# The low part of split weights, made by a negation on ScalarE and an accumulating transfer instead of subtractions

## The chip, the cores and the metric

The kernel runs on one core of a Trainium2 chip. The metric is the device time of one execution in microseconds. The engines are named as the profile names them: PE (TensorE, with PEld for its weight loads), DVE (VectorE), ACT (ScalarE), POOL (GpSimd) and SP (SyncE, which here only issues transfers).

## What is computed

The reference is one inference step of a two-layer hybrid backbone over 128 context tokens and 512 latent tokens, 640 in all, with D = 1024 and a feed-forward width of 2816. Every layer runs four token mixers on the same normalised input, merges them through gates, projects, and runs a SwiGLU feed-forward:

```python
h = _rmsnorm(x, lp['norm1_g']) * (1.0 + sc1) + sh1
(aq, ak, av, az, aa, ab, ..., mg) = jnp.split(h @ lp['w_in'], offs, axis=-1)
...                                      # four mixers: DeltaNet, differential attention, HGRN2, neighbourhood attention
proj = jnp.einsum('btnw,nwd->btnd', branches, lp['w_branch'])
gates = jax.nn.sigmoid(mg.reshape(bsz, t, N_BRANCH, D_MODEL))
out = jnp.einsum('btnd,btnd->btd', gates, proj) @ lp['w_out']
x = x + g1 * out
h = _rmsnorm(x, lp['norm2_g']) * (1.0 + sc2) + sh2
x = x + g2 * (jax.nn.silu(h @ wg) * (h @ wu)) @ wd
```

All of it is in 32-bit floats. The change concerns the weights of these products: `w_in`, `w_branch`, `w_out`, `wg`, `wu` and `wd`.

## The kernel before

**Split products.** TensorE multiplies in a reduced format (F32R). So each operand is split in two, a high part (the value rounded to that format) and a low part (the value minus its high part), and a product is the sum of three matmuls: high by high, high by low of the activations, low of the weights by high. `unit` does that for one half of the tokens (320 columns) and up to 8 steps of 128 rows: 24 matmuls of 320 columns for one weight tile of 128x1024. `units` does both halves at once. Activations are kept split (`hh`, `hl`, `fa`, `mo`, `mgs`); weights are streamed.

**Weights.** `load_w` brings one weight tile: a transfer on SP's queue into `wraw` (2 buffers), the copy to the high part `whi` on ACT (3 buffers), and the low part `wlo` (3 buffers, `NLO`) as a subtraction. In the mixers (`self.weaving`) the last 416 of 1024 columns (`PC`) are subtracted on POOL and the first 608 on DVE; elsewhere DVE does all of it. `load_spare` does the same into other tiles for a few weights that have to be kept, and is not touched. The callers of `load_w` are `first` (three tiles of the opening), `a_small` (`in_wab`, 128 columns), `store_fm` and `store_tok` (the input projection, the latter with two tiles held at a time), `pregate` and `merge` (gates and branch projections), the loop over `in_wo` in `build` (the output projection, one tile for each half of the tokens), and `ffn` (`up`: gate and up tiles of 1024 columns; `down`: tiles of 512 columns, in one chunk 256).

**Order.** In the mixers TensorE's order is written out by a planner (`weave`), which puts steps of the mixers' chains between the matmuls of the projections; it is part of the program and is not changed at run time. The other engines' orders are made by a scheduler from priorities; what `load_w` issues has a high one (`WPRI`). Each engine and each issuing queue works strictly in its order. POOL's queue also carries transfers of the differential attention (`rr`, `rx`, `bqk`, `bqt`, `bKd`), SP's queue nearly all others.

**Stages.** For each layer: the mixers with the input projection, then the output projection, then the feed-forward, where `up` of one chunk of columns is followed by `down` of the chunk before it. The first layer begins with `first`; the modulation of the second layer is computed on DVE during the first layer's feed-forward.

Of the kernel before, what the change touches and what calls it, by code (L numbers as in the profile page):

```python
# [12 lines left out]
ALU = mybir.AluOpType  # L13
# [24 lines left out]
WPRI, WCUT = 550000, 1024  # L38
QB = 1
RE = 0  # L40
PC = 416
DPRI = 0
QM, QD = 1, 0
VC = 1
# [69 lines left out]
class Net:  # L114
# [58 lines left out]
    def weave(self, chains, fill, side):  # L173
# [25 lines left out]
        while chains or fill or side:  # L199
            first = None  # L200
            for group, margin in ((side, 0.0), (chains, SLACK), (fill, 0.0)):
                pick = None
                for c in group:
                    t = ready(c)
                    if t is not None:
                        if t + margin <= self.now:
                            pick = c
                            break
                        first = t + margin if first is None else min(first, t + margin)
                if pick is None:  # L210
                    continue
                if group is chains:
                    self.chain, self.rank = True, pick[2]
                    with self.tc.high_priority(offset=100000 * (8 - self.rank)):
                        step(pick, group)
                    self.chain = False
                else:

                    group.insert(0, group.pop(group.index(pick)))
                    step(pick, group)  # L220
                break
            else:
                assert first is not None, "chains wait for each other"
                self.now = first
# [50 lines left out]
            lo.append(l)  # L275
        return Halves(hi, 512), Halves(lo, 512)

    def load_w(self, src, n=1024, pc=0, raw=None):

        if raw is None:  # L280
            raw = self.wraw.tile([128, 1024], F32, tag="raw", name="wraw")
        with self.tc.high_priority(offset=DPRI):
            self.nc.sync.dma_start(raw[:, :n], src)
        hi = self.whl.tile([128, 1024], F32R, tag="hi", name="whi")
        lo = self.whl.tile([128, 1024], F32R, tag="lo", name="wlo", bufs=NLO)
        with self.tc.high_priority(offset=WPRI):
            m = n - (PC if self.weaving and n == 1024 else pc)
            self.a.copy(hi[:, :n], raw[:, :n])
            self.v.tensor_tensor(lo[:, :m], raw[:, :m], hi[:, :m].bitcast(F32), ALU.subtract)
            if m < n:  # L290
                self.g.tensor_tensor(lo[:, m:n], raw[:, m:n], hi[:, m:n].bitcast(F32), ALU.subtract)
        return hi, lo
# [223 lines left out]
    def first(self, xs, mod, ms_):  # L516
# [11 lines left out]
        wide, wa, shifts, ws = [], [], {}, []  # L528
# [31 lines left out]
                    v.tensor_tensor(accs[j], accs[j], sq, ALU.add)  # L560
        for m in ms_:
            raw = self.mo.tile([128, 2, T], F32, tag="mo", name="wa0").rearrange("p a b -> p (a b)") if len(ws) == 2 else None
            ws.append(self.load_w(self.I['win'][0, m], pc=512, raw=raw))
        w1 = []
        for n in range(8):
            w1.append(self.SA("wa2"))
# [81 lines left out]
        n = 0  # L648
# [1308 lines left out]
```

## Time and profile before

| | |
|---|---|
| Median of 3 runs | 3494.56 us (3494.28 to 3498.4) |
| The profiled execution | 3495.59 us, of which the span is 3493.6 us |
| Mean granted clock of TensorE | 0.984 of full speed |
| PE busy | 3368.8 us (96 %) |
| DVE busy | 2352.5 us (67 %) |
| ACT busy | 1422.4 us (41 %) |
| POOL busy | 544.5 us (16 %) |
| Transfers | 460.16 MB, mean 132 GB/s |

Busy time is the time in which an engine executes an instruction; issuing a transfer is not counted. The span runs from the first instruction to the last; the 2.0 us around it belong to the execution as a whole. The mixers of the first layer run to about 1210 us, its output projection from 1231 to 1288, its feed-forward to about 1770; the second layer's mixers end at about 2920 and its feed-forward at the end.

### The profile page before, as it was taken

The page shows a single profiled execution, that of the slowest core. Times are in us where ns is not written, and L with a number is a line of the kernel's source. Part 1 is how long each engine was busy: PE and PEld are TensorE (multiplying, and loading weights), DVE is VectorE, ACT ScalarE, POOL GpSimd, SP SyncE. Part 2 cuts the span into 40 slices and gives each one's busy share as a digit, 9 for nine tenths or more (in the row PEclk, how much of TensorE's full clock was granted, in tenths as well). Part 3 has the DMA queues.
Part 4 walks back from the last instruction along what each step waited for, and adds up shares of the span by engine and source line. Part 5 has one row for each costly group of instructions (what it writes and reads, how often), then busy time and mean ns, then how long its engine had stood idle before and what let it go on. Part 6 is the DMA issues. An engine that isn't in the chain of part 4 may idle for free. (4 is left out here: it accounts for less than half of the span.)

```text
span 3493.6 us, 63588 instructions
## 1 busy us (share of the span) xinstructions
PE 3368.8 (96%) x23932; PEld 3298.6 (94%) x23932; DVE 2352.5 (67%) x5497; ACT 1422.4 (41%) x3170; POOL 544.5 (16%) x592
## 2 busy tenths in 40 slices
PE   8999999989999999999999999999999999999998
PEld 5989999988999999999999899999999999999998
DVE  7689888865676478887456797777555646633435
ACT  5344444544543353222253455445544433522222
POOL 2221112422122100000002212124122121000000
PEclk9999999999999999999999999999999999999999
DMA  6444333855454254444244333348453235322222
GB/s 218 151 145 139 115 110 124 242 178 159 131 154 126 95 177 147 151 153 131 76 131 148 130 115 112 103 127 244 141 150 120 87 100 161 106 67 79 74 84 67
DMA packets 297931, 460.16 MB, mean 132 GB/s; under 512 B 48148, under 2 KB 193172, under 8 KB 297624
## 3 DMA queue, kind: packets, MB, share of 16 engines
q1 hardware_dynamic: 286296, 423.58, 39.3%
q0 software_dynamic: 11328, 32.52, 3.1%
q8 instruction: 189, 3.10, 0.4%
q14 instruction: 118, 0.97, 0.1%
HBM read 368.42 MB, written 87.56 MB: 131 GB/s over the span
## 5 line engine op out<-in xcount | busy, mean ns | idle before, releaser
L152 PE MATMUL pu<-hh,whi 128*128 128x320 f32 (+1 forms) x3760 | 1094.7, 319 | 18.1 <-ACT stg L107 14.9
L152 PE MATMUL pu<-hl,whi 128*128 128x320 f32 (+1 forms) x3760 | 1064.8, 311 | 2.2 <-DVE hl L107 2.2
L152 PE MATMUL pu<-hh,wlo 128*128 128x320 f32 (+1 forms) x3760 | 1065.2, 311 | 0.0
L107 ACT CAST whi<-wraw 128x1024 fp32r<-128x1024 f32 (+2 forms) x410 | 391.1, 954 | 898.0 <-PE pu L152 492.6
L152 PEld LDWEIGHTS pu<-hh,whi 128*128 128x128 f32 (+1 forms) x3760 | 683.9, 189 | 23.3 <-ACT stg L107 15.7
L152 PEld LDWEIGHTS pu<-hl,whi 128*128 128x128 f32 (+1 forms) x3760 | 684.3, 189 | 4.5 <-DVE hl L107 2.5
L152 PEld LDWEIGHTS pu<-hh,wlo 128*128 128x128 f32 (+1 forms) x3760 | 682.5, 188 | 1.7
L107 DVE TENSOR_TENSOR wlo<-wraw,whi 128x608 fp32r<-128x608 f32 (+3 forms) x410 | 389.7, 951 | 314.2 <-ACT whi L107 309.4
L107 POOL TENSOR_TENSOR wlo<-wraw,whi 128x416 fp32r<-128x416 f32 (+1 forms) x209 | 325.5, 1558 | 1761.1 <-ACT whi L107 1539.8
L152 PE MATMUL pu<-mo,whi 128*128 128x320 f32 x1024 | 236.5, 318 | 5.4 <-DVE mo L107 3.4
L152 PE MATMUL pu<-fa,whi 128*128 128x320 f32 x1152 | 215.6, 309 | 0.0
L107 DVE SCALAR_TENSOR_TENSOR x<-pu,gn,x 128x128 f32<-128x128 f32 (+1 forms) x336 | 133.8, 435 | 93.3 <-PE pu L152 92.4
L152 PE MATMUL ptk<-whi,hh 128*128 128x256 f32 x640 | 193.9, 303 | 0.0
L512 DVE CUSTOM_DVE_ANT_0 junk<-wa,cs,mod 128x256 bf16<-128x256 f32 (+1 forms) x288 | 172.7, 600 | 25.6 <-DMA wa<-in_wada 20.7
L152 PE MATMUL ptk<-wlo,hh 128*128 128x256 f32 x640 | 183.5, 287 | 3.2 <-DVE wlo L107 3.2
L152 PE MATMUL ptk<-whi,hl 128*128 128x256 f32 x640 | 183.4, 287 | 0.0
L152 PEld LDWEIGHTS pu<-mo,whi 128*128 128x128 f32 x1024 | 174.5, 193 | 7.6 <-DVE mo L107 4.9
L152 PEld LDWEIGHTS pu<-fa,whi 128*128 128x128 f32 x1152 | 180.8, 188 | 0.0
L152 PE MATMUL pu<-mo,wlo 128*128 128x320 f32 x512 | 160.7, 314 | 0.0
L152 PE MATMUL pu<-fa,wlo 128*128 128x320 f32 x576 | 131.1, 309 | 0.0
L152 PEld LDWEIGHTS ptk<-wlo,hh 128*128 128x128 f32 x640 | 125.2, 196 | 3.4 <-DVE wlo L107 3.4
L152 PEld LDWEIGHTS ptk<-whi,hh 128*128 128x128 f32 x640 | 125.5, 196 | 0.0
(422 smaller groups left out, 6092.1 us busy)
## 6 DMA issues: line engine op xcount, KB each, us to landing
wraw<-in_win SPq DMA_DIRECT2D x151, 512.0 KB, 3.9
wa<-in_wada SPq DMA_DIRECT2D x116, 256.0 KB, 3.0
wraw<-in_wg SPq DMA_DIRECT2D x44, 512.0 KB, 3.5
wraw<-in_wu SPq DMA_DIRECT2D x44, 512.0 KB, 3.7
wraw<-in_wd SPq DMA_DIRECT2D x80, 256.0 KB, 2.6
p<-stg SPq DMA_DIRECT2D x112, 160.0 KB, 2.9
wa<-in_wada SPq DMA_DIRECT2D x128, 128.0 KB, 2.5
wraw<-in_wtok SPq DMA_DIRECT2D x32, 512.0 KB, 3.8
```

The lines of the kernel that those rows point to most:

```text
L107: r = f(*args, **kw)
L152: r = self.nc.tensor.matmul(out, lhsT, rhs, start=start, stop=stop)
L512: self.nc.vector.tensor_tensor_reduce(junk, raw, cs[g], 0.5, o if k0 else self.bada[:, l, m:m + 1], ALU.mult, ALU.add, o)
```

## The change

`load_w` gets a second way, used by all callers but `first`. ACT writes the negated weights into the low tile, which rounds them to F32R, so the tile holds minus the high part. A transfer issued by POOL then reads the same weights from DRAM once more and adds them to the tile. ACT's copy to the high part stays. The constant `PC` is gone, since neither DVE nor POOL subtracts in this way.

```diff
-PC = 416
...
-    def load_w(self, src, n=1024, pc=0, raw=None):
+    def load_w(self, src, n=1024, pc=0, raw=None, add=True):
...
+        if add:
+            with self.tc.high_priority(offset=WPRI):
+                self.a.mul(lo[:, :n], raw[:, :n], -1.0)
+                self.nc.gpsimd.dma_start(lo[:, :n], src, accum_op=ALU.add)
+                self.a.copy(hi[:, :n], raw[:, :n])
+            return hi, lo
         with self.tc.high_priority(offset=WPRI):
-            m = n - (PC if self.weaving and n == 1024 else pc)
+            m = n - pc
...
-            ws.append(self.load_w(self.I['win'][0, m], pc=512, raw=raw))
+            ws.append(self.load_w(self.I['win'][0, m], pc=512, raw=raw, add=False))
```

408 tiles take the new way: 326 of 1024 columns, 64 of 512, 16 of 256 and 2 of 128, together 189.9 MB. TensorE's order is the same up to the first layer's output projection. ACT's order at the beginning of that projection, before (`mgh` are the last of the merged activations, `sq` the squares for the next norm, `wraw` here the tiles of `in_wo`):

```order
L107 CAST mgh_14778<-mrg_11837 128x320
L107 CAST whi_14860<-wraw_14858 128x1024
L107 CAST mgh_14779<-mrg_11837 128x320
L107 CAST whi_14895<-wraw_14893 128x1024
L107 ACTIVATE sq_15067<-x_14786 128x320
L107 CAST whi_14930<-wraw_14928 128x1024
L107 ACTIVATE sq_15069<-x_14821 128x320
```

ACT at the same place now:

```order
L106 CAST whi_14863<-wraw_14861 128x1024
L106 ACTIVATE wlo_14864<-wraw_14861 128x1024
L106 CAST mgh_14780<-mrg_11838 128x320
L106 CAST whi_14899<-wraw_14897 128x1024
L106 ACTIVATE wlo_14900<-wraw_14897 128x1024
L106 ACTIVATE sq_15076<-x_14787 128x320
L106 CAST whi_14935<-wraw_14933 128x1024
L106 ACTIVATE wlo_14936<-wraw_14933 128x1024
```

Each copy to a high part now has the negation of the same tile right behind it, and the work of the norm stands behind both. POOL's order in the first layer's mixers, where it issues the transfers of the differential attention, before:

```order
L163 DMA bqt_7740<-bqk0_102 64x4x128 x2
L163 DMA bKd_7737<-bqk0_102 128x512
L163 DMA bKd_7738<-bqk0_102 128x512
L107 MEMSET dpr_7760 128x256
L163 DMA rr_7518<-qk2_96 32x2x512 x2
L107 TENSOR_TENSOR wlo_8063<-wraw_8060,whi_8062 128x416
L107 TENSOR_TENSOR wlo_8186<-wraw_8183,whi_8185 128x416
L107 TENSOR_TENSOR wlo_8339<-wraw_8336,whi_8338 128x416
L163 DMA bqk2_104<-rr_7518 64x512 x4
L163 DMA rr_7536<-qk3_97 32x2x512 x3
```

POOL at the same place now:

```order
L162 DMA bqt_7741<-bqk0_102 64x4x128 x2
L162 DMA bKd_7738<-bqk0_102 128x512
L162 DMA bKd_7739<-bqk0_102 128x512
L106 MEMSET dpr_7761 128x256
L162 DMA rr_7519<-qk2_96 32x2x512
L288 DMA wlo_8064<-in_win 128x1024
L162 DMA rr_7519<-qk2_96 32x2x512 x2
L288 DMA wlo_8187<-in_win 128x1024
L288 DMA wlo_8340<-in_win 128x1024
L162 DMA bqk2_104<-rr_7519 64x512 x4
```

The accumulating transfers stand about where POOL's subtractions stood, between the same transfers of the attention. In the output projection and the feed-forward, where POOL did nothing before, its queue now holds one such transfer for each tile.

## Rows read from the trace of the kernel before

**Rows 1.** The page's busy line: busy us (share of the span) x instructions.

```profile
PE 3368.8 (96%) x23932; PEld 3298.6 (94%) x23932; DVE 2352.5 (67%) x5497; ACT 1422.4 (41%) x3170; POOL 544.5 (16%) x592
```

**Rows 2.** Waits of PE: who waited for whom, us in total, times, longest.

```profile
PE pdt L158 <- ACT dPl L107: 15.3, 5, 6.5
...
PE pCT L158 <- DVE C L107: 8.0, 5, 2.9
...
PE ptk L152 <- DVE wlo L107: 3.2, 1, 3.2
...
PE pao L152 <- ACT ow L107: 0.4, 1, 0.4
...
PE pu L152 <- DVE spl L107: 0.2, 1, 0.2
```

**Rows 3.** Stretches: length, busy us of PE, PEld, DVE, ACT, POOL; clock, DMA share, GB/s.

```profile
200.00:400.00 200.00, 183.78 (x1395) 179.03 (x1394) 174.29 (x402) 97.33 (x216) 38.79 (x48) 0.97 0.42 134
2300.00:2500.00 200.00, 190.80 (x1409) 189.10 (x1409) 133.94 (x281) 102.42 (x249) 64.46 (x80) 0.97 0.62 182
1259.00:1288.00 29.00, 29.00 (x201) 28.75 (x200) 21.23 (x44) 14.20 (x25) 0.00 (x0) 1.00 0.41 132
1400.00:1500.00 100.00, 100.00 (x684) 100.00 (x683) 80.21 (x190) 23.13 (x40) 0.00 (x0) 1.00 0.49 151
3100.00:3200.00 100.00, 100.00 (x683) 100.00 (x683) 37.75 (x72) 22.39 (x38) 0.00 (x0) 1.00 0.24 72
...
1213.00:1219.00 6.00, 5.40 (x20) 0.50 0.79 253
...
2402.00:2410.00 8.00, 8.00 (x52) 0.86 1.10 321
```

**Rows 4.** Groups by shape: busy us, mean ns of one, idle before and its causes.

```profile
L107 ACT CAST whi<-wraw 128x1024 fp32r<-128x1024 f32 x328 | 344.1, 1050 | 611.6 <-PE pu L152 311.6 <-issue 248.3 <-PE ptk L152 20.0
L107 ACT CAST whi<-wraw 128x512 fp32r<-128x512 f32 x64 | 39.8, 623 | 241.1 <-PE pu L152 163.8 <-issue 77.4
L107 ACT CAST whi<-wraw 128x256 fp32r<-128x256 f32 x16 | 6.5, 409 | 44.2 <-issue 22.6 <-PE pu L152 16.1 <-DMA wraw<-in_wd 4.2
L107 DVE TENSOR_TENSOR wlo<-wraw,whi 128x608 fp32r<-128x608 f32 x207 | 189.9, 917 | 148.2 <-ACT whi L107 145.8 <-PE pdv L158 1.1 <-DMA wa<-in_wada 0.2
L107 POOL TENSOR_TENSOR wlo<-wraw,whi 128x416 fp32r<-128x416 f32 x207 | 322.9, 1560 | 1759.7 <-ACT whi L107 1538.5 <-issue 33.0 <-DVE mrg L107 23.9
```

**Rows 5.** Timeline of ACT, start and length in us: projection, gate and up, down.

```profile
1254.26 1.05 ACT L107 CAST whi<-wraw 128x1024 fp32r<-128x1024 f32 x1 [2.10 <-PE pu L152]
...
1257.77 1.05 ACT L107 CAST whi<-wraw 128x1024 fp32r<-128x1024 f32 x1 [2.10 <-PE pu L152]
...
3174.29 1.05 ACT L107 CAST whi<-wraw 128x1024 fp32r<-128x1024 f32 x1 [5.31 <-issue]
3181.33 1.05 ACT L107 CAST whi<-wraw 128x1024 fp32r<-128x1024 f32 x1 [5.33 <-issue]
...
3223.53 0.62 ACT L107 CAST whi<-wraw 128x512 fp32r<-128x512 f32 x1 [2.90 <-PE pu L152]
3227.05 0.62 ACT L107 CAST whi<-wraw 128x512 fp32r<-128x512 f32 x1 [2.90 <-PE pu L152]
```

**Rows 6.** Transfers: issuing queue, count, KB each, median us from issue to landing.

```profile
wraw<-in_wg SPq DMA_DIRECT2D x44, 512.0 KB, 3.5
wraw<-in_wd SPq DMA_DIRECT2D x80, 256.0 KB, 2.6
rx<-qk POOLq DMA_DIRECT2D x8, 512.0 KB, 5.3
wraw<-in_wd SPq DMA_DIRECT2D x16, 128.0 KB, 2.1
rot<-in_rcos POOLq DMA_DIRECT2D x2, 256.0 KB, 3.7
```

**Rows 7.** Issues of one tile by POOL: ns min/median/max, first and last start.

```profile
L163 POOL DMA_DIRECT2D bqt<-bqk x64: 619/627/653, 672.4 to 2808.5; - x64
```

## The prediction

> **What bounds the kernel now.** I read the busy line first: TensorE works 3368.8 of 3493.6 us [rows 1], so only some 125 us lie idle and the rest is matmuls that the change does not touch. Then the waits of TensorE [rows 2]: 25 pairs in which it waits for VectorE, from 8.0 us down to 0.2, add up to 62.8 us, and 14 for ScalarE, from 15.3 down to 0.4, to 47.4 us. Weights are almost never late: one wait of 3.2 us for a low part. Then the stages [rows 3]: in the mixers TensorE is busy 184 and 191 of 200 us, with VectorE at 174 and 134; in the output projection and the feed-forward it is gapless, with VectorE at 38 to 80 of 100. So VectorE matters in the mixers alone, and anywhere else a saved subtraction is worth nothing. Last, the clock: from 1213 to 1219 us it was granted at 0.50, its lower level of 1.2 GHz, right after TensorE had waited; 20 matmuls took the 6 us that some 41 take at the upper level [rows 3, 5]. [...]
>
> **What is removed.** 408 low parts lose their subtraction. In the mixers 207 of them cost VectorE 0.917 us and GpSimd 1.560 us each [rows 4], 190 us and 323 us. GpSimd's share lay beside other work. VectorE's is about 9 % of what it does there.
>
> **What is added on ScalarE.** 408 negations. They have the tile and length of the copy to the high part: 1050 ns (326 tiles of 1024 columns), 623 ns (64), 409 ns (16) [rows 4], 390 us in all. Copy and negation stand next to each other, mostly copy first. In the gapless stages ScalarE is idle most of the time (22 of 100 us busy, 14 of 29 in the projection) [rows 3], so the work costs no time but lengthens the path of a tile by one step. In the mixers ScalarE goes from 97 to some 116 of 200 us.
>
> **What is added on the queues.** 408 issues by GpSimd. The 64 issues of bqt took 619 to 653 ns [rows 7], so 408 take about 260 us, less than the subtractions that left the same engine. An issue waits for the negation, and GpSimd's other transfers of the mixers (bqt, bKd, rr) queue behind it; they queued behind the subtraction before, which waited for the copy, so this wait is longer by one negation only. GpSimd has no other work in the feed-forward.
>
> **How long the accumulating transfer takes.** No row shows one. From below: a plain load of 512 KB by SP lands in 3.5 us [rows 6]. Nearest: GpSimd's own load of 512 KB (rx) lands in 5.3 us. An addition must also read the tile that it adds to, one more pass of the same bytes; between 128 and 512 KB a load goes from 2.1 to 3.5 us, so a pass of 512 KB costs 1.9 us. I take 5.3 + 1.9 = 7.2 us; for 256 KB 3.7 (rot) + 0.9 = 4.6; for 128 KB 3.7. From above: each of two extra passes (read, write) as long as a whole load, 5.3 + 2 x 3.5 = 12.3 us.
>
> **The new path of a tile.** There are three buffers each for high and low parts. The pair that TensorE leaves after tile i is refilled for tile i+3, which is needed two tiles later. Before: copy and subtraction, some 2.4 us. Now: 0.1 hand-over + copy + negation + landing = 0.1 + 2.1 + 7.2 = 9.4 us for 1024 columns, 0.1 + 1.25 + 4.6 = 6.0 for 512, 0.1 + 0.8 + 3.7 = 4.6 for 256. What TensorE has to cover it is two tiles' work, from the distance of successive copies [rows 5]: 2 x 7.04 = 14.1 us in the gate and up products (covered, even at 14.5 nearly), 2 x 3.52 = 7.0 in the projection and in the down products of 512 columns, 2 x 1.76 = 3.5 for those of 256 columns (12 matmuls instead of 24).
> - Output projection, 32 tiles: by latency (9.4 - 7.0) / 3 = 0.8 us a tile, 26 us. By rate: a tile now makes 512 KB pass three times (load, addition's source, addition's destination), 1573 kB; the stretch at 132 GB/s has a DMA share of 0.41, so 322 GB/s at full share, and 2402 to 2410 us indeed shows 321 GB/s [rows 3]. 1573 / 322 = 4.9 us a tile against 3.5, 1.37 x 32 = 44 us. The slower limit counts: 44 us (0 if the landing is 3.5 and the addition counts once; 80 at 12.3).
> - From down back to gate, 4 times a layer: the first gate tile has only two down tiles to hide in, 9.4 - 7.0 = 2.4 us, times 8 = 19 us (0 to 60).
> - Down tiles of 512 columns, 64: 6.0 against 7.0, nothing (70 at the upper end, where the landing is 3.7 + 2 x 2.6 = 8.9).
> - Down tiles of 256 columns, 16: (4.6 - 3.5) / 3 x 16 = 6 us (0 to 30).
> - Token products directly after token products, twice a layer: two tiles are held to the end and the next pair's second one starts late. It is needed some 2.5 us into the pair and ready after 9.4 - 1.3 us, 5.6 us late; chain steps between cover part. 2.5 x 4 = 10 us (0 to 36).
> - First tile behind the opening (in_wab): nothing hides its addition, 4 us (2 to 6).
> - Mixers, engines: ScalarE 20 % more, VectorE 9 % less, on waits of 47.4 and 62.8 us: +9 - 5 = +4 us (-31 to +40).
> - Mixers, DMA: 207 tiles in some 2370 us are 46 GB/s, twice that beside 134 and 182 GB/s [rows 3]; the shares of 0.42 and 0.62 rise to about 0.7 and 0.9, and the chains' own loads land later. +10 us (0 to 40). In the feed-forward of the first layer 0.49 rises to some 0.95: just carried.
> - Clock: two more falls among these stalls, 6 us (0 to 40).
>
> Sum 44 + 19 + 6 + 10 + 4 + 4 + 10 + 6 = 103 us. On the profiled execution, 3495.6 us (1.0 above the median of 3494.56), that is 3599; against the median 3598.
>
> **A rule weighed.** The issues of bqt, spread over stretches with VectorE 67 to 87 % busy, all took 619 to 653 ns [rows 3, 7]: nothing held them up. The Trainium skill, SBUF — State Buffer, section "Who interferes with whom", says that GpSimd can't write the descriptors of its transfers while VectorE runs an operation in a two-port mode, and gives 620 ns that become 3100. By that rule some 2.5 us would come on top of each addition that meets such an operation, 52 and 39 us in the first two terms and about 3626 in all; the row decides, and I give it no chance of its own.
>
> **The rivals.**
> Hidden and faster (0.20). Place: the mixers. If the addition lands within 4.8 us, 2.2 + 4.8 is covered by the 7.0 of the projection and all latency terms vanish. Then what counts is VectorE's queue: half of the 62.8 us behind it gone and some 5 us of low clock with it, -36; the opening and the token pairs leave +8 or so. 3496 - 28 = 3468. For it: VectorE at 174 of 200 us, copies that are short. Against it: 5.3 us for rx already, without an addition, and ScalarE on the same chains.
> Evened out (0.07): latency terms of some 25 us against that gain, about 3495.
> Slow additions (0.09). The landing is at the upper end, 12.3 us. Then 80 + 60 + 70 + 30 + 36, 10 in the gate and up products and some 40 in the mixers, 326: about 3822. Against it: rx moves as many bytes in 5.3 us.
> That the change does not do what it says: the order of the changed kernel shows 408 additions and only the opening's three tiles with subtractions; no chance given.
>
> **How the numbers follow.** My forecast, 3598, has 0.64, and its own range is 3505 to 3740 from the bounds above (not all at their end together). Two runs of this kernel can be told apart from about 0.2 %, 7 us. Faster: 0.20. Same: 0.07. Slower: 0.64 + 0.09 = 0.73. The range 3465 to 3740 leaves out the slow additions and the outer tails, about 2 in 10.
>
> **What would show it.** The landing of wlo from in_wo and in_wg: 7.2 us expected; near 4.8 or less the latency terms fall, over 9 the down products starve too. In the projection copies 4.9 us apart instead of 3.52, the DMA share at its top. TensorE waiting for a transfer into wlo, 8 times at the return to gate tiles. VectorE some 390 us less busy, ScalarE 390 us more, with the gate and up products still 7.04 us a tile. I am wrong if TensorE's waits for wlo sum to under 20 us, or if the mixers alone take up more than 40 us either way.

## The result, and the profile after

The changed kernel takes 3719.49 us (median of 4 runs, 3713.86 to 3723.44) against 3496.05 for the kernel before (4 runs, 3494.28 to 3498.4): a ratio of 1.0639, 95 % interval 1.0625 to 1.0653. It is slower by 223 us, and by 224 between the two profiled executions that are read below; the forecast was slower by 103.

The busy line and the busiest queues of the page after (queue: packets, MB, share of 16 transfer engines over the span):

```profile
span 3717.8 us, 63685 instructions
PE 3436.2 (92%) x23932; PEld 3346.9 (90%) x23932; DVE 1951.6 (52%) x5089; ACT 1750.8 (47%) x3576; POOL 564.7 (15%) x793
q1 hardware_dynamic: 286296, 423.58, 36.8%
q0 software_dynamic: 70080, 222.47, 32.1%
```

The same two queues before:

```profile
q1 hardware_dynamic: 286296, 423.58, 39.3%
q0 software_dynamic: 11328, 32.52, 3.1%
```

Against [rows 1] TensorE runs the same 23932 matmuls but is busy 67.4 us longer, nearly all of it by the clock (its mean over the span falls from 0.984 to 0.966), and it idles 156.8 us more. VectorE lost 401 us of work, ScalarE gained 328. The share of GpSimd's queue in the transfer engines' time rose by 29 points (an engine-us is one us of one of the 16): 0.321 x 16 x 3717.8 - 0.031 x 16 x 3493.6 = 17,360 engine-us for 190 MB, or 91 for a MB. The transfers of the other queue held the engines as long as before, 0.393 x 16 x 3493.6 = 21,970 and 0.368 x 16 x 3717.8 = 21,890 engine-us: their packets did not get slower.

Where the time went, by stage. The stretches run from the first matmul of a stage to that of the next (that of the first projection before starts at 1243.6 us, not at the 1231 named ahead); columns as in [rows 3] (the second last is the transfer engines' share). Before, then after, each in the order mixers, projection, feed-forward of the first layer and of the second:

```profile
0.00:1243.60 1243.60, 1175.25 (x8399) 1130.59 (x8400) 923.93 (x2333) 565.03 (x1332) 277.37 (x305) 0.97 0.49 151
1243.60:1301.90 58.30, 58.30 (x401) 58.05 (x400) 43.72 (x85) 32.55 (x59) 0.00 (x0) 1.00 0.46 147
1301.90:1772.60 470.70, 469.33 (x3197) 467.96 (x3197) 348.11 (x818) 127.59 (x222) 0.17 (x3) 1.00 0.45 139
1772.60:2951.10 1178.50, 1135.19 (x8333) 1114.09 (x8332) 779.71 (x1730) 544.94 (x1290) 266.95 (x284) 0.98 0.43 131
2951.10:3009.40 58.30, 58.30 (x402) 58.05 (x400) 43.72 (x85) 32.58 (x59) 0.00 (x0) 1.00 0.46 146
3009.40:3493.60 484.20, 472.38 (x3211) 469.85 (x3210) 213.34 (x447) 119.70 (x211) 0.00 (x0) 0.99 0.25 75
```

```profile
0.00:1308.70 1308.70, 1188.48 (x8400) 1140.93 (x8401) 798.39 (x2225) 657.17 (x1438) 205.47 (x308) 0.96 0.70 185
1308.70:1387.00 78.30, 66.30 (x399) 64.02 (x399) 26.93 (x69) 45.35 (x73) 12.07 (x14) 0.91 0.85 209
1387.00:1892.70 505.70, 483.85 (x3198) 478.36 (x3197) 279.25 (x736) 188.24 (x309) 73.36 (x88) 0.97 0.79 193
1892.70:3141.20 1248.50, 1156.69 (x8334) 1131.03 (x8333) 674.24 (x1625) 637.14 (x1393) 191.15 (x287) 0.97 0.65 167
3141.20:3213.80 72.60, 61.53 (x401) 58.14 (x400) 26.80 (x69) 45.38 (x73) 12.04 (x14) 1.00 0.92 225
3213.80:3717.80 504.00, 479.31 (x3211) 474.43 (x3209) 146.03 (x367) 177.51 (x293) 70.59 (x82) 0.98 0.62 135
```

Length minus busy is idle time, and busy time beyond that of before is put down to the clock (roughly: in the second layer's projection the clock reads 1.00 and TensorE is still busy 3.2 us longer):

| stage | longer by | of it idle | of it clock |
|---|---|---|---|
| mixers, both layers | 135.1 us | 100.4 | 34.7 |
| output projections | 34.3 | 23.1 | 11.2 |
| feed-forwards | 54.8 | 33.4 | 21.4 |

The mixers took the largest part. The waits of TensorE after, columns as in [rows 2]:

```profile
PE pdt L157 <- ACT dPl L106: 25.9, 6, 8.9
PE pu L151 <- DMA wlo<-in_wg: 24.9, 10, 3.9
PE pu L151 <- DMA wlo<-in_wo: 23.0, 17, 3.4
...
PE ptk L151 <- DMA wlo<-in_wtok: 14.8, 5, 5.6
...
PE pu L151 <- DMA wlo<-in_wd: 7.9, 8, 3.9
...
PE pu L151 <- DMA wlo<-in_wab: 3.0, 1, 3.0
```

Seven pairs that wait for a low part sum to 76.6 us (3.2 before). But the pairs that wait for ScalarE doubled too, from 47.4 to 100.5 us, and those for VectorE, which has less to do, rose from 62.8 to 77.1: the mixers' own chains got slower. Their transfers show why that may be. Columns as in [rows 6], after:

```profile
wlo<-in_wo POOLq DMA_DIRECT2D x32, 512.0 KB, 8.0
wlo<-in_wd POOLq DMA_DIRECT2D x64, 256.0 KB, 4.7
wlo<-in_wd POOLq DMA_DIRECT2D x16, 128.0 KB, 3.2
p<-stg SPq DMA_DIRECT2D x112, 160.0 KB, 5.7
bqt<-bqk POOLq DMA_DIRECT2D x64, 128.0 KB, 7.5
```

The last two belong to the mixers and are the same instructions as before, when they landed in:

```profile
p<-stg SPq DMA_DIRECT2D x112, 160.0 KB, 2.9
bqt<-bqk POOLq DMA_DIRECT2D x64, 128.0 KB, 5.2
```

### The profile page after: what moved, and what is told of

Read it like the earlier page. It is cut to its first block, busy times and chain, and to the rows that moved or that the text cites. A ratio compares the mean times of both kernels' runs of the same rounds, so it can differ in the third digit from the quotient of the medians.

```text
span 3717.8 us, 63685 instructions
## 1 busy us (share of the span) xinstructions
PE 3436.2 (92%) x23932; PEld 3346.9 (90%) x23932; DVE 1951.6 (52%) x5089; ACT 1750.8 (47%) x3576; POOL 564.7 (15%) x793
## 4 chain that ended last, share of the span: by engine, by line
PE 37%; issue 33%; DMA 15%; DVE 6%; POOL 5%; ACT 3%; SPq 1%; POOLq 0%; DVEq 0%; ACTq 0%
PE pu L151 23%; POOL wlo L288 4%; PE ptk L151 3%; DMA craw<-p 2%; DMA wa<-in_wada 1%; DMA wlo<-in_wg 1%; PE pdv L151 1%; PE pW L151 1%; DMA wraw<-in_win 1%; PE pX L151 1%; PE pbo L151 1%; PE pbs L151 1%; DMA wlo<-in_wo 1%; DVE cacc L106 1%; PE pT L151 1%
## 5 line engine op out<-in xcount | busy, mean ns | idle before, releaser
L151 PE MATMUL pu<-hh,whi 128*128 128x320 f32 (+1 forms) x3760 | 1107.3, 322 | 20.3 <-ACT stg L106 16.9
L151 PE MATMUL pu<-hh,wlo 128*128 128x320 f32 (+1 forms) x3760 | 1076.7, 314 | 30.9 <-DMA wlo<-in_wg 24.9
L151 PEld LDWEIGHTS pu<-hh,wlo 128*128 128x128 f32 (+1 forms) x3760 | 691.6, 191 | 36.5 <-DMA wlo<-in_wg 27.5
L151 PEld LDWEIGHTS pu<-hh,whi 128*128 128x128 f32 (+1 forms) x3760 | 694.1, 192 | 26.7 <-ACT stg L106 18.7
L151 PEld LDWEIGHTS pu<-hl,whi 128*128 128x128 f32 (+1 forms) x3760 | 694.1, 192 | 6.2 <-DVE hl L106 4.2
L106 ACT ACTIVATE wlo<-wraw 128x1024 fp32r<-128x1024 f32 (+3 forms) x408 | 391.1, 959 | 52.2 <-PE ptk L151 14.1
L288 POOL DMA_DIRECT2D wlo<-in_win x146 | 129.4, 886 | 1239.4 <-ACT wlo L106 928.2
L517 DVE CUSTOM_DVE_ANT_0 junk<-wa,cs,mod 128x256 bf16<-128x256 f32 (+1 forms) x288 | 164.4, 571 | 65.9 <-DMA wa<-in_wada 61.6
L151 PE MATMUL ptk<-wlo,hh 128*128 128x256 f32 x640 | 183.9, 287 | 14.8 <-DMA wlo<-in_wtok 14.8
L106 DVE SCALAR_TENSOR_TENSOR fs<-fs,pu 128x320 f32<-128x320 f32 x88 | 39.3, 484 | 206.8 <-ACT fs L106 206.7
```

What stands on the lines that cost most here:

```text
L106: r = f(*args, **kw)
L151: r = self.nc.tensor.matmul(out, lhsT, rhs, start=start, stop=stop)
L288: self.nc.gpsimd.dma_start(lo[:, :n], src, accum_op=ALU.add)
L517: self.nc.vector.tensor_tensor_reduce(junk, raw, cs[g], 0.5, o if k0 else self.bada[:, l, m:m + 1], ALU.mult, ALU.add, o)
```

## The experiments

What was to be told apart: is it the work moved to ScalarE, the low parts that come late, the transfer engines that the additions share with everybody, or GpSimd's queue, on which attention's transfers stand behind the additions? Times are medians, the interval is that of the ratio to the kernel before on the same chip.

### Which stages: the change in one part alone

```diff
 # f_only: outside the mixers alone          m_only: "if add and self.weaving:"
-        if add:
+        if add and not self.weaving:
```

The rest is split by subtraction as before, with `PC` put back.

> The addition is used only outside the mixers; in the mixers the weights are subtracted as before. By the stages of the two traces the output projections took 34 us more and the feed-forwards 55, so if the stages add up: 3496 + 89 = 3585. If the mixers' 135 us are partly the aftermath of the feed-forward, less than 3496 + 89 is not possible here and m_only shows less than 135.

> The addition is used only in the mixers. If the stages add up: 3496 + 135 = 3631, with the projection and the feed-forward as before (58 us and 471 or 484 us).

Measured: f_only 3584.26 us (1.0248, 1.0228 to 1.0267), m_only 3635.87 us (1.0400, 1.0374 to 1.0426). The losses, 88 and 140 us, add up to the whole within 5 us, so the mixers can be studied alone.

### ScalarE's work

```diff
 # m_act: the kernel before, and in the mixers also
+            if self.weaving:
+                self.a.mul(lo[:, :n], raw[:, :n], -1.0)
 # neg_dve: the kernel after, its negation on VectorE
-                self.a.mul(lo[:, :n], raw[:, :n], -1.0)
+                self.v.tensor_scalar(lo[:, :n], raw[:, :n], -1.0, None, ALU.mult)
```

In m_act the subtraction overwrites the negation, so only its cost is left.

> The kernel before, with the negation on ScalarE alone added in the mixers: it writes the low tile, which the subtractions then overwrite. No transfer is added and VectorE keeps its work. Theory ScalarE (the chains of the mixers wait for ScalarE because 207 more instructions of 1.05 us stand in its order): most of the 135 us, at least 60. Theory transfers (the chains' own loads and stores land later beside 108 MB more): 10 to 25 us, as ScalarE has room.

> The changed kernel with the negation on VectorE instead of ScalarE, everywhere. ScalarE is then as busy as before, VectorE about as before. Theory ScalarE: the mixers lose at least 60 of their 135 us, about 3650. Theory transfers: within 25 us of 3719.

Measured: m_act 3511.69 us (1.0052, 1.0035 to 1.0070), so all of ScalarE's additional work in the mixers costs 16 us. neg_dve 3700.41 us (1.0591, 1.0572 to 1.0610), 19 us less than after. Neither comes near 135: ScalarE is not the main cause.

### Late low parts

```diff
 # lo4: the kernel after with
-NS, NSA, NRAW, NLO = 4, 18, 2, 3
+NS, NSA, NRAW, NLO = 4, 16, 2, 4
```

A fourth buffer lets each negation and addition begin one tile earlier. Its memory comes from `NSA`, so sa16 is the kernel before with `NSA` 16.

> The changed kernel with four low tiles instead of three (room from 16 buffers in sa): the negation and the addition of a tile now start one tile earlier than its copy to the high part. Theory late weights in the projection and the feed-forward: the waits for wlo there (56 us, and the clock falls behind them) nearly vanish; what is left is the rate of the projection, some 10 to 40 of 89 us, so about 3719 - 60 = 3660 if the mixers stay, about 3600 if the mixers suffer from late weights as well.

> The kernel before with 16 instead of 18 buffers of the pool sa, which makes room for one more tile of 4 KB a partition. A control for m_dma and lo4: all theories expect it within 10 us of before.

Measured: sa16 3495.43 us (0.9991, 0.9981 to 1.0001), lo4 3647.84 us (1.0424, 1.0391 to 1.0456), between its two expected times. Being in time is worth 72 us: 34 of them in the mixers (2523.0 us both against 2557.2), 33 in the feed-forwards, and only 3 in the projections (148.2 against 150.9), which speaks for the transfer engines as their limit and not for the latency of one tile. The mixers of lo4, columns as in [rows 3]:

```profile
0.00:1294.10 1294.10, 1187.89 (x8399) 1138.25 (x8400) 795.16 (x2222) 656.77 (x1437) 207.15 (x309) 0.96 0.71 188
1857.50:3086.40 1228.90, 1152.19 (x8333) 1127.16 (x8332) 667.13 (x1623) 638.08 (x1391) 190.75 (x288) 0.97 0.67 171
```

What TensorE still waits for low parts is little, 22 us in all and 1.2 of it in the mixers (`in_win`), and yet 152 us are lost, 101 of them in the mixers:

```profile
PE pu L151 <- DMA wlo<-in_wo: 10.6, 7, 3.1
PE pu L151 <- DMA wlo<-in_wg: 5.0, 4, 2.1
...
PE pu L151 <- DMA wlo<-in_win: 1.2, 1, 1.2
```

### The addition against a plain transfer

```diff
 # plain: the kernel after with
-                self.nc.gpsimd.dma_start(lo[:, :n], src, accum_op=ALU.add)
+                self.nc.gpsimd.dma_start(lo[:, :n], src)
```

The subtraction is left out here: the low tiles hold the weights themselves. Orders, waits, bytes from DRAM and ScalarE's work are those of the kernel after.

> The changed kernel with the second transfer as a plain load instead of an accumulating one: the low tiles hold the weights themselves, so the low-part products are of other values. Same order, same waits, same bytes from DRAM; the reading of the tile is left out. If the addition counts twice: landing falls from 7.7-8.0 to about 5.5 us for 512 KB, the projection is no longer bound by rate, and the total falls by about half of the 224, to 3600. If the addition costs as much as a load: within 30 of 3719.

Measured: 3539.62 us (1.0110, 1.0091 to 1.0129). A plain transfer in the addition's place gives back 180 of the 223 us, more than either expectation (mixers 2458.1 us, 36 over before). Its rows (queue, then landings):

```profile
q0 software_dynamic: 70080, 222.47, 19.7%
...
p<-stg SPq DMA_DIRECT2D x112, 160.0 KB, 4.8
...
wlo<-in_wo POOLq DMA_DIRECT2D x32, 512.0 KB, 4.9
...
bqt<-bqk POOLq DMA_DIRECT2D x64, 128.0 KB, 5.9
```

The same bytes hold the engines 0.197 x 16 x 3538.5 - 1733 = 9,420 engine-us, where 1733 is the queue's time before; the additions held them 17,360, 1.84 times as long. The Trainium skill, Collectives: The Full Stack, "The bandwidth ceiling: the fold count and why AG ≠ RS ≠ AR", says of collectives that the reducing transfer needs two source reads where the copying one needs one and so reaches about half its rate, with 1.93 as the measured ratio; the 1.84 here agrees nearly.

So two things hang on the addition, its latency and its engine time, and lo4 has shown that the latency is the smaller one. The next runs load the mixers of the kernel before with transfers that nobody waits for.

### Spare transfers, first try

```diff
 # m_dma: sa16, in the mixers, for each weight tile
+            if self.weaving:
+                self.nc.gpsimd.dma_start(self.spill[:, :n], src, accum_op=ALU.add)
```

> The kernel before, with 16 buffers as in sa16, and in the mixers an accumulating transfer of every weight tile into a spare tile that nobody reads. Subtractions, ScalarE and the path of a weight are as before; only the transfer and its issue on GpSimd are added. Theory transfers (the chains' loads and stores land later): most of the mixers' 135 us less what VectorE's relief gave back, at least 70 above sa16. Theory late weights (the tile's longer path and GpSimd's queue standing behind it): at most 30 above sa16.

Measured: 4018.87 us (1.1488, 1.1468 to 1.1508), and no answer. The transfer depends on no other work, so the scheduler put all of them (209, with the two of `in_wab`) into the first layer's mixers, each behind the one before it on the one spare tile, and GpSimd's queue stood still for them, 931 us in all, most of it here:

```profile
POOL spill L289 <- DMA spill<-in_win: 631.8, 128, 8.3
```

The first layer's mixers grew to 1763.9 us, the second's, which held none, stayed at 1181.9.

### Spare transfers tied to the tiles

```diff
 # m_spare_add: sa16, behind GpSimd's subtraction of each tile    (m_spare_pln: without accum_op)
+                if self.weaving:
+                    sp = self.spill[self.nsp & 1]
+                    self.nsp += 1
+                    self.nc.gpsimd.tensor_copy(sp[:, :1], lo[:, n - 1:n].bitcast(F32))
+                    self.nc.gpsimd.dma_start(sp[:, :n], src, accum_op=ALU.add)
```

The copy of one column makes the transfer wait for its tile. Both entries of `spill` are one tile here.

> The kernel before (NSA 16, which alone moved nothing: 0.9991), weights still split by subtractions, and in the mixers GpSimd, right after its own subtraction of each weight tile, also issues an accumulating transfer of that tile's 512 KB into one spare tile that nobody reads. No matmul, and no chain of the mixers, waits for a spare transfer; they can only be hurt through shared transfer engines or through GpSimd's queue. Theory 'shared' (about 100 of the mixers' 135 us come from what the additions do to the transfers and the queue of the others): the mixers' two stages grow by 80 to 110 us together, 3580 to 3605 us. Theory 'late weights' (the loss is the matmuls' and the scheduler's wait for the low parts themselves): no more than 20 us, 3495 to 3515 us.

> As m_spare_add, with a plain transfer of the same 512 KB into the spare tile in place of the accumulating one: the same orders, the same queue, the same bytes landed, without the addition's second reading. If the engines' time is what hurts, about a quarter of m_spare_add's loss (as the plain kernel kept 37 us of the mixers' 135): 3515 to 3525 us. If GpSimd's queue is what hurts, through the issues themselves, the loss stays near that of m_spare_add.

Measured: m_spare_add 3666.47 us (1.0473, 1.0442 to 1.0504), m_spare_pln 3555.05 us (1.0172, 1.0152 to 1.0191). Additions that no matmul reads cost 170 us, more than either theory said and more than the mixers lose in the kernel after; plain ones cost 59, also more than expected (20 to 30). The late low parts can't be the whole story: the weights are not later here, TensorE waits for one low part 2.4 us (3.2 before). But in m_spare_add the queue stood still as well, if less, 188 us in all, most of it here:

```profile
POOL spill L295 <- DMA spill<-in_win: 134.2, 47, 6.7
```

### GpSimd's queue or the shared engines

```diff
 # qsp: the kernel after, qsp_b: the kernel before, m_spare_q: m_spare_add, each with
-QB = 1
+QB = 0
-QM, QD = 1, 0
+QM, QD = 0, 0
```

This takes attention's and the rotation's transfers off GpSimd's queue.

> The kernel after with the mixers' own transfers that stand on GpSimd's queue (attention's q, k and bias tiles and the rotation's: constants QB and QM 0) moved to SyncE's queue. Theory 'GpSimd's queue' (these stand behind additions that wait for their negation): most of the mixers' unexplained 100 us comes back, 3630 to 3660 us. Theory 'shared engines': their landings stay long, 3700 to 3730 us. Compare with qsp_b for what the move itself does.

> The kernel before with the same move of attention's and the rotation's transfers from GpSimd's queue to SyncE's, as the control of qsp. Both theories: within 15 us of before, 3485 to 3510 us, since GpSimd's queue carries no weights there.

> m_spare_add (one spare tile) with attention's and the rotation's transfers on SyncE's queue, so that nothing the chains load stands behind a blocked addition; compare with qsp_b (3544 us). Theory 'shared engines': 140 to 175 us over qsp_b, 3685 to 3720 us. Theory 'GpSimd's queue': under 70 us over qsp_b, below 3614 us.

Measured: qsp 3764.9 us (1.0767, 1.0740 to 1.0794), qsp_b 3543.98 us (1.0134, 1.0112 to 1.0155), m_spare_q 3688.9 us (1.0555, 1.0538 to 1.0573). The move costs by itself 48 us, which I had not expected: SyncE's queue carries the weights, and their loads now stand behind attention's transfers. TensorE waits three times for a high part, once for 30.6 us, behind a stretch in which SyncE issued no weight between 2382.24 and 2446.64 us. The wait and that issue in qsp_b:

```profile
PE pu L152 <- ACT whi L107: 72.3, 3, 30.6
```

```profile
2446.64 0.45 SPq L283 DMA_DIRECT2D wraw<-in_win  x1
```

On top of that the change still costs 221 us (qsp over qsp_b) and the spare additions 145. With none of the chains' transfers on GpSimd's queue the loss stays: it isn't that they stand behind the additions there. In m_spare_q the queue still stood still, 224 us in all; m_spare2 below takes that away.

### Doses of engine time

The pools of small (`NGS` 5, `NSA` 15, otherwise the kernel before) hold two spare tiles, so that a transfer waits for the one two tiles earlier. m_spare2 adds 512 KB to one of them for each tile of the mixers, m_spare2h half of it, m_spare2p loads 512 KB plainly, and m_spare2pp does so twice.

```diff
 # m_spare2: the lines of m_spare_add on small, two spare tiles; m_spare2p: without accum_op
 # m_spare2h:
+                    self.nc.gpsimd.dma_start(sp[:, :512], src[:, :512], accum_op=ALU.add)
 # m_spare2pp: m_spare2p and behind it
+                    self.nc.gpsimd.tensor_copy(self.spill[self.nsp & 1][:, :1], lo[:, n - 1:n].bitcast(F32))
+                    self.nc.gpsimd.dma_start(self.spill[self.nsp & 1][:, :n], src)
```

> The kernel before with smaller pools (NGS 5, NSA 15), which makes room for two spare tiles: the control of m_spare2 and m_spare2h. Both theories: within 10 us of before, 3486 to 3506 us.

> small, with m_spare_add's spare accumulating transfers turned over two spare tiles, so that an issue waits for the addition two tiles earlier, not for the last one, and GpSimd's queue hardly stands still. Theory 'shared engines': the loss stays, 130 to 175 us over small. Theory 'GpSimd's queue': it falls to that of the plain spare transfer or below, under 70 us over small.

> As m_spare2, with each spare addition cut to the tile's first 512 columns: 256 KB in place of 512 KB, the same number of issues and copies on GpSimd. Theory 'shared engines': about half of m_spare2's loss, 60 to 90 us over small. Theory 'GpSimd's queue' (issues): the loss of m_spare2 nearly whole.

> m_spare2 with a plain transfer of 512 KB into the spare tiles in place of the addition; compare with small (3491.5 us). Theory 'engine time alone': as m_spare2h, whose spare transfers hold the engines about as long, 85 to 110 us over small. Theory 'an addition has a price beyond the engines' time': as m_spare_pln, 45 to 70 us over small.

> m_spare2p with a second plain transfer of the same 512 KB into the other spare tile behind the first, so that the engines are held about as long as by m_spare2's additions. Theory 'engine time alone': about m_spare2's loss, 190 to 230 us over small. Theory 'an addition has a price beyond the engines' time': about twice the single plain dose, 100 to 140 us over small.

Measured, with the engine time worked out from the queue's row as above, less that of small (1787):

| kernel | us | ratio, interval | over small | engine-us of the spare transfers | us for 1000 |
|---|---|---|---|---|---|
| small | 3491.54 | 0.9989, 0.9980 to 0.9999 | | | |
| m_spare2p | 3578.91 | 1.0228, 1.0206 to 1.0249 | 87 | 4,910 | 17.8 |
| m_spare2h | 3588.38 | 1.0267, 1.0247 to 1.0287 | 97 | 5,220 | 18.5 |
| m_spare2pp | 3666.72 | 1.0478, 1.0455 to 1.0501 | 175 | 9,700 | 18.1 |
| m_spare2 | 3707.74 | 1.0602, 1.0578 to 1.0627 | 216 | 9,770 | 22.1 |

The queue's row of small, m_spare2p and m_spare2h, in this order:

```profile
q0 software_dynamic: 11328, 32.52, 3.2%
...
q0 software_dynamic: 41136, 141.06, 11.7%
...
q0 software_dynamic: 41136, 86.80, 12.2%
```

The rows of m_spare2 (queue, the spare transfer, two of the chains' transfers, and all that its issue waits for an earlier spare addition):

```profile
q0 software_dynamic: 41136, 141.06, 19.5%
...
spill<-in_win POOLq DMA_DIRECT2D x143, 512.0 KB, 7.8
...
p<-stg SPq DMA_DIRECT2D x112, 160.0 KB, 4.2
...
bqt<-bqk POOLq DMA_DIRECT2D x64, 128.0 KB, 7.3
```

```profile
POOL spill L295 <- DMA spill<-in_win: 1.1, 1, 1.1
```

The queue's row of m_spare2pp, where p<-stg lands in 4.1 us and bqt in 6.6 (3.0 and 4.9 in small):

```profile
q0 software_dynamic: 70944, 249.60, 19.5%
```

Two of the waits of the chains for a transfer, in small:

```profile
DVE cacc L107 <- DMA craw<-p: 32.6, 13, 5.3
...
ACT mo L107 <- DMA moT<-oT: 19.8, 22, 2.3
```

and in m_spare2:

```profile
DVE cacc L107 <- DMA craw<-p: 75.4, 15, 10.4
...
ACT mo L107 <- DMA moT<-oT: 59.4, 22, 5.7
```

In m_spare2 the queue no longer stands still for its spares (1.1 us), and the loss didn't fall, it is the largest. Half the bytes by addition, or all of them plainly, hold the engines about as long and cost about the same; twice the plain dose costs twice. m_spare2pp also doubles GpSimd's issues, and its queue stood still 147 us for spares; m_spare2, without either, loses 41 us more, so these two don't make the loss. It goes by the engines' time, about 18 us for 1000 engine-us, though no matmul reads these transfers. The chains' waits go the same way: ScalarE and VectorE together stood idle 145 us in small until a transfer other than a weight had landed, and 220, 226, 288 and 330 us in the four runs in the table's order.

It is not a proven straight line. The full additions cost some 40 us above it (216 against 18 x 9.77 = 176), and from m_spare2h to m_spare2, with the same issues, the step is 26 us for 1000. The expectations were met by m_spare2p alone (85 to 110): m_spare2 and m_spare2h came out above theirs, m_spare2pp between its two. And no run has the issues and the one-column copies without a transfer: VectorE is 52 to 64 us busier in the mixers of all four than in small (1707 us), so a part of each loss may be theirs. The step from m_spare2h to m_spare2, 119 us, has both alike and is free of it.

## Why the prediction was wrong in size

The measured 3719 us lie inside the forecast's own range of 3505 to 3740. That is luck: two terms, the mixers' transfers and the clock, went past their ends, and the others stayed near their middle.

**What bounds the kernel before** held: TensorE's matmuls are the floor, VectorE matters in the mixers alone, and outside them only the new path could cost.

**What is removed, and ScalarE's work** held. VectorE fell by 401 us (390 forecast), 231 of them in the mixers (190); the negations are a group of 391.1 us (390), of which ScalarE's busy time shows 328, since a negation starts before the copy ahead of it has ended. m_act puts their price in the mixers at 16 us, where I had +9; what VectorE's relief gave back there was not measured.

**The accumulating transfer** was sized nearly right: landings of 7.7 to 8.0 us (7.2 forecast), 4.7 for 256 KB (4.6), 3.2 for 128 KB (3.7). It loads the engines 1.84 times as long as the same bytes by a plain transfer (2 assumed). The issues took some 356 us in all instead of 260, with means of 861 to 890 ns for tiles of 1024 columns and 1482 ns as the longest one; no row shows a cost of that.

**Output projection**: 34 us against 44. The pace in it is the forecast one. Copies on ScalarE come at 4.93 us a tile over three tiles (14.78 / 3; 4.9 forecast, 3.52 before in [rows 5]) where the buffers have run out, but in bunches (the two between start at 1328.11 and 1331.62):

```profile
1324.58 1.05 ACT L106 CAST whi<-wraw 128x1024 fp32r<-128x1024 f32 x1 [6.41 <-PE pu L151]
...
1339.36 1.05 ACT L106 CAST whi<-wraw 128x1024 fp32r<-128x1024 f32 x1 [5.37 <-PE pu L151]
```

The engines' share of 0.85 and 0.92 over the two stages and lo4's gain of only 3 us bear out that their rate counts there rather than the latency. (The 321 GB/s that stood for full share came at a share of 1.10, which makes 292 at 1.0 and 5.4 us a tile; the 4.9 measured lie nearer to the 322 used.) Three tiles a layer that are fetched ahead would account for 8 of the 10 us of difference (6 x 1.4); no run separated that.

**Return from down to gate**: of the 10 waits for `in_wg`, 8 are these returns, 20.0 us against 19; the other two, 4.9 us, come right behind the projections, where the forecast had no term. **Token after token**: 14.8 against 10. **Opening**: 3.0 against 4. These three steps were right in mechanism and near in size. **Down tiles**: 7.9 us against 6, but by luck. The tiles of 256 columns, for which the 6 stood, made TensorE wait 2.4 us; those of 512, put at nothing, 5.5, of which 4.9 in one stretch (1605 to 1623 us) in which ScalarE also waited for the plain loads of `in_wd`. Gate and up tiles stayed 7.04 us apart (copies at 3375.85, 3382.89 and 3389.93 us of after).

**The step that failed is "Mixers, DMA"**, taken at 10 us with 40 as its end. The mixers lost 135 us. Taking off what the steps above name there (token 14.8, opening 3.0) and the mixers' part of the clock (34.7), some 83 us of idle time remain where the two terms for the mixers had 14; in lo4, where TensorE hardly waits for low parts in the mixers, they are still 101 us longer than before. I had worked out that the engines' share would rise to 0.7 and 0.9 in the two stretches of [rows 3] (it is 0.62 from 200 to 400 us and 0.78 from 2420 to 2620, and 0.70 and 0.65 over the two mixers) and that the chains' loads would land later, and then priced that as a small disturbance, though no row gave a price. The spare transfers show one at such shares (0.68 and 0.64 in m_spare2): 207 additions whose result nobody reads cost 170 to 216 us. The chains go to DRAM and back at many steps: p<-stg takes 5.7 instead of 2.9 us, bqt 7.5 instead of 5.2, and ScalarE and VectorE together stand idle 301 us instead of 120 until a transfer other than a weight has landed. That such delays add up along a chain is how I read these rows; no run took one chain apart. By the forecast's own words, "if the mixers alone take up more than 40 us", it failed there.

That the mixers of the kernel after lose 135 us and not the 170 to 216 of the spare additions is not settled by a run. VectorE does 231 us less in them, which plain suggests is worth something: its 207 transfers cost 36 us in the mixers, where m_spare2p's cost 87. But the orders differ too, so that gain, my rival's 36 us, was only argued.

**The clock**, 6 us forecast, took some 67: the same matmuls are busy that much longer. I had paid for two more falls in all. It follows the idle time (156.8 us more), at some 0.43 us for each, so it was missed along with the mixers and, in the feed-forward, beside steps sized right: 21.4 us of clock on 33.4 of waits.

**The rivals** "hidden" and "evened out" fell with the landing of 7.7 to 8.0 us; "slow additions" fell since the landing wasn't 12.3, though the total lies about halfway between the forecast and it, for another reason. Nor did the gain that "hidden" counted on show: with landings of 4.5 to 5.4 us plain was still some 40 us slower than before.

No kernel tried here beats the one before; small and sa16 lie within 0.2 % of it.

## What to carry to other kernels

Price a new transfer twice: by the wait of whoever reads it, and by the engine time that it takes from everybody else; where chains of small transfers through DRAM are on the path, the second can be the larger even at a mean share of 0.5 to 0.7. To find it, add the transfer into a tile that nobody reads, tied to the work it belongs to, vary its bytes, and run the issues alone as well. And add to each new wait of TensorE what its clock takes afterwards: here some 40 % on top.

## What the runs showed of the hardware

- An accumulating transfer from DRAM held the transfer engines 1.84 times as long as a plain one of the same bytes from the same queue (17,360 and 9,420 engine-us for 190 MB; 1.99 times between the spare transfers of m_spare2 and m_spare2p), and 512 KB landed in 7.7 to 8.0 us instead of 4.5 to 5.4.
- Its issue by GpSimd took 862 ns, against 529 for the plain one (means of the 42 issues of `in_wg` in after and in plain).
- Transfers on another queue land later beside the additions, at a mean share of 0.7: p<-stg on SyncE's queue takes twice as long (2.9 to 5.7 us), while the other queue's packets held the engines as long as before (21,970 and 21,890 engine-us).
- SyncE's queue is a resource of its own: moving attention's transfers onto it cost 48 us, with 72.3 us of waits of TensorE for high parts.
